# Dense projections issued as whole groups: a priority block around 21 of the 24 matmuls of each group

## The chip, the core and the metric

One core of one Trainium2 chip runs the whole program. The metric is the device time of one execution in microseconds, the median of several runs. The core has five engines that work side by side, each through its own queue in order: TensorE (PE) for matmuls, VectorE (DVE), ScalarE (ACT), GpSimd (POOL) and SyncE (SP), which here issues most of the DMAs. TensorE writes its results to PSUM, eight banks of 2 KB for each of 128 partitions; the other data lies in SBUF or in the chip's main memory.

## What is computed

The reference is one inference step of a two-layer decoder. Each layer normalises the hidden state, multiplies it by one input projection of 4108 columns, gives the columns to four mixers of four heads each, and multiplies the mixed result by an output projection:

```python
proj = jnp.einsum('btd,de->bte', hn, w_in_l)
...
s_hgrn, o_a = run_mixer(chunk_vector_decay, step_vector_decay, ...)
...
s_gdn, o_b = run_mixer(chunk_gated_delta, step_gated_delta, ...)
...
s_ssd, o_c = run_mixer(chunk_scalar_decay, step_scalar_decay, ...)
...
s_ret, o_d = run_mixer(chunk_scalar_decay, step_scalar_decay, ...)
...
y = jnp.concatenate([y_a, y_b, y_c, y_d], axis=-1)
out = jnp.einsum('bte,ed->btd', y, w_out_l)
```

The prompt has 2048 tokens behind 16 learned ones; eight sample sequences of one token each run beside it with states of their own. The four mixers are recurrences over tokens: HGRN2 (a), the gated delta rule (b), Mamba-2 (c) and retention (d). All data is 32-bit.

## The kernel before

Tokens stand in 17 tiles: tile 0 holds the 16 learned tokens and the eight samples in 40 rows, the others 128 tokens each. Two tiles make a block (the first block has tile 0 as well), and there are eight blocks. A layer runs in five stages, each a loop over blocks or tiles:

- `mixC` (Mamba-2), blocks 0 to 7.
- `denseB` (the projections of the gated delta rule), blocks 0 to 7, with `prepB` after every second block. Beside it the walk starts: `walkB`, a generator that carries the gated-delta state over all 65 pieces of 32 tokens. Each piece (`stepB`) is a chain: a read of the state on PE (`wo`), an addition on DVE (`wz`, line 1212), an update on PE (`tr<-wz,bkt`), and the new state on DVE (`sbd`, line 312), on which the next read waits. `hook` puts the next step of the walk into the program at set places of the stages.
- `mixA` (HGRN2), blocks 0 to 7, with the rest of the walk beside it. After the projections of a block come eight rounds of score matmuls (`sc<-aq,ak`, line 235 by way of `scores`), up to 64 matmuls of 64 x 32 in a round; between two rounds DVE scales `aq` and `ak` in place (lines 792 and 793).
- `mixD` (retention), blocks 0 to 7. Its outputs take their PSUM bank in turn from the pools `po` and `pwo`; the walk holds the one buffer of `pwo` for a tile at a time.
- `outproj`, tiles 0 to 16.

Each projection is exact to nearly full precision through three matmuls on parts: the weights and the activations are split into a high and a low part, and high x high, high x low and low x high are added up in PSUM. Over the contraction of 1024 in eight steps this makes a group of 24 matmuls into one PSUM buffer; the pool `pd` has two of them. `dense_cm` (lines 478 to 487) computes 128 columns for a whole block of 256 or 296 tokens, `dense_rows` (489 to 496) up to 512 columns for one tile; it is called by `dense_tm` and `outproj`. Behind a group its eviction follows, which reads the PSUM buffer.

The order of the instructions on each engine is not the program's. A planner lays it down beforehand, engine by engine: whenever an engine is free in the planner's own timing, it takes, of the instructions whose inputs are there, the one of the lowest rank. The rank is the running number in the program. Inside `tc.high_priority(offset=n)` the rank is that number less n, and the instructions of such a block do not move the running number on: the first one after it continues where the block began. Evictions, weight loads and `prepB` stand in `early()`, which is an offset of 3000 (line 194); some small GpSimd steps have 6000 (`POFF`). On the chip each engine then runs its queue in that order.

The core of a group, before:

```python
for d in range(8):
    T.matmul(ps, hi[:, d], b.xh[:, d, 0:b.n], start=(d == 0), stop=False)
    T.matmul(ps, hi[:, d], b.xl[:, d, 0:b.n], start=False, stop=False)
    T.matmul(ps, lo[:, d], b.xh[:, d, 0:b.n], start=False, stop=(d == 7))
with early():
    evict(full[:, 0:4 + b.n] if raw else ps)
```

Of the kernel before, what the change touches and what calls it, by code (L numbers as in the profile page):

```python
# [92 lines left out]
def body(tc, ctx, a, o, nch, depth, blks, off):  # L93
    nc = tc.nc
    V, S, G, T = nc.vector, nc.scalar, nc.gpsimd, nc.tensor
# [97 lines left out]
    def early():  # L193
        return tc.high_priority(offset=3000)

    def ptile(pool, tag):
        return pool.tile([128, 512], F32, tag=tag, name=tag)
# [280 lines left out]
    def dense_cm(w, b, evict, raw=False):  # L478
        hi, lo = w
        full = ptile(pd, "pd")  # L480
        ps = full[:, 4:4 + b.n]
        for d in range(8):
            T.matmul(ps, hi[:, d], b.xh[:, d, 0:b.n], start=(d == 0), stop=False)  # L483
            T.matmul(ps, hi[:, d], b.xl[:, d, 0:b.n], start=False, stop=False)  # L484
            T.matmul(ps, lo[:, d], b.xh[:, d, 0:b.n], start=False, stop=(d == 7))  # L485
        with early():
            evict(full[:, 0:4 + b.n] if raw else ps)

    def dense_rows(ps, R, pcs, xh, xl):
        nd, n = pcs[0][0].shape[1:3]  # L490
        for d in range(8):
            hi, lo = (x[:, d % nd] for x in pcs[d // nd])
            T.matmul(ps[0:R, 0:n], xh[:, d], hi, start=(d == 0), stop=False)  # L493
            T.matmul(ps[0:R, 0:n], xh[:, d], lo, start=False, stop=False)  # L494
            T.matmul(ps[0:R, 0:n], xl[:, d], hi, start=False, stop=(d == 7))  # L495
        return ps[0:R, 0:n]

    def dense_tm(pcs, b, evict):
        for t in b.tiles:
            R, x0 = rows(t), b.col[t]  # L500
            r = dense_rows(ptile(pd, "pd"), R, pcs, b.xh[:, :, x0:x0 + R], b.xl[:, :, x0:x0 + R])
            with early():
                evict(t, r)
# [29 lines left out]
    def dense_z(ws, b):  # L533
        z = blk("z")
        for p in range(2):
            dense_cm(ws[p], b, lambda ps: silu2(ps, z[:, p, 0:b.n], b.n))
        return z
# [173 lines left out]
    def mixA(L, W, b):  # L711
# [4 lines left out]
        for p in range(2):  # L716
            dense_cm(wq[p], b, lambda ps: silu2(ps, q[:, p, 0:n], n))
            hook(rA)
        for p in range(2):
            def evf(ps):  # L720
                th = we("th")
                act(th[:, 0:n], ps, AF.Tanh, scale=0.5)
                fo = f[:, p, 0:n]
                act(kk[:, p, 0:n], th[:, 0:n], AF.Identity, scale=L.lc[:, 4 + p:5 + p], bias=L.lc[:, 2 + p:3 + p])
                V.tensor_scalar(fo, th[:, 0:n], L.lc[:, 2 + p:3 + p], L.lc[:, p:p + 1], ALU.mult, ALU.add)
                V.tensor_scalar(fo, fo, TINY, None, ALU.max)
            dense_cm(wff[p], b, evf)
            hook(rA)
# [881 lines left out]
    def outproj(L, W, t, Ln, between=None):  # L1610
        R = rows(t)
        y = f4([128, 8, 128], "yf")
        nc.sync.dma_start(y[:, :, 0:R], ydr[t])
        yh, yl = xpair((NT - t) % 2, 128)
        S.copy(yh[:, :, 0:R], y[:, :, 0:R])
        tt(yl[:, :, 0:R], y[:, :, 0:R], f32(yh[:, :, 0:R]), ALU.subtract)
        hx = f4([128, D], "hx")
        load_h(L.l, t, hx)
        for qd in range(2):
            ps = dense_rows(ptile(pd, "pd"), R, W[qd], yh[:, :, 0:R], yl[:, :, 0:R])  # L1620
            cs = slice(512 * qd, 512 * qd + 512)
            tt(hx[0:R, cs], hx[0:R, cs], ps, ALU.add)  # L1622
            if between:
                with early():
                    next(between)
                    Wn = next(between)
        if Ln is not None:
            nc.sync.dma_start(hdr[t], hx[0:R])
            xprep(Ln, t, hx)
            if between:  # L1630
                return Wn
        else:
            stt(hx[0:R], hx[0:R], rms_scale(hx, R), fnw[0:R], ALU.mult, ALU.mult)
            if t == 0:
                nc.sync.dma_start(o["y_sample"].rearrange("b o d -> (b o) d"), hx[32:40])
            else:
                nc.sync.dma_start(o["y_prompt"][0, 128 * (t - 1):128 * t, :], hx)
# [158 lines left out]
```

## Time and profile before

| | us |
|---|---|
| median of three runs | 2864.69 (2863.39 to 2867.74) |
| the profiled execution | 2857.64 |
| its span, first to last instruction | 2855.9 |
| PE busy | 2734.7 |
| PE weight loads busy | 2483.6 |
| DVE busy | 1694.0 |
| ACT busy | 1010.5 |
| POOL busy | 1057.8 |

The page gives the busy time of each engine, its costliest groups of instructions and what ended the idle time ahead of them. The windows view gives the same by stretch of time, the timeline gives single instructions with start and length. Matmuls are pipelined, so a matmul of 0.28 us may have its successor start 0.12 us later; what the stream costs is read from the distance of starts.

### The profile page before, as it was taken

The numbers are of one execution on the slowest core, as the hardware profiler recorded it, in microseconds if no ns is written. First come the engines' busy times: TensorE is split into PE (matmuls) and PEld (weight loads), VectorE is DVE, ScalarE is ACT, GpSimd is POOL, SyncE is SP. The second block draws the span as 40 slices with busy tenths as digits, with TensorE's granted clock in tenths as the row PEclk, the third lists the DMA queues.
The fourth block names the chain that finished last, engine by engine and source line by source line (L and its number), as shares of the span: only waits on it lengthen the run. The fifth ranks groups of instructions, "written<-read, shape, count | busy, mean of one in ns | idle before, by whom it ended". The sixth has DMA issues, their size and how long they took to land. (4 is left out here: it accounts for less than half of the span.)

```text
span 2855.9 us, 72831 instructions
## 1 busy us (share of the span) xinstructions
PE 2734.7 (96%) x29492; PEld 2483.6 (87%) x29492; DVE 1694.0 (59%) x4756; ACT 1010.5 (35%) x2547; POOL 1057.8 (37%) x2032
## 2 busy tenths in 40 slices
PE   6989999989999999999988999899999999999998
PEld 6889898989889888888878999899988898888887
DVE  5777766655666745454456767656566657444533
ACT  4545532333333412232244445233333333222321
POOL 4454546557323221110033535646763322212100
PEclk9999999999999999999999999999999999999999
DMA  7243445563232423237772424534632223322443
GB/s 181 66 141 108 146 136 151 155 160 104 69 111 72 132 73 112 77 111 210 223 216 81 143 92 123 144 119 142 185 97 86 74 97 97 97 96 72 146 140 111
DMA packets 385175, 349.69 MB, mean 122 GB/s; under 512 B 144313, under 2 KB 349617, under 8 KB 374601
## 3 DMA queue, kind: packets, MB, share of 16 engines
q1 hardware_dynamic: 381320, 335.96, 38.3%
q0 software_dynamic: 3520, 9.09, 1.6%
q8 instruction: 233, 3.82, 0.5%
q14 instruction: 102, 0.83, 0.1%
HBM read 247.06 MB, written 98.10 MB: 121 GB/s over the span
## 5 line engine op out<-in xcount | busy, mean ns | idle before, releaser
L483 PE MATMUL pd<-xh,wh 128*128 128x256 f32 (+1 forms) x2816 | 825.7, 293 | 25.3 <-DVE hB L907 10.4
L484 PE MATMUL pd<-xl,wh 128*128 128x256 f32 (+1 forms) x2816 | 813.1, 289 | 0.0
L485 PE MATMUL pd<-xh,wl 128*128 128x256 f32 (+1 forms) x2816 | 811.8, 288 | 0.9 <-DVE wl L458 0.7
L483 PEld LDWEIGHTS pd<-xh,wh 128*128 128x128 f32 x2816 | 539.4, 192 | 43.1 <-issue 18.9
L493 PE MATMUL pd<-wh,xh 128*128 128x512 f32 (+5 forms) x1632 | 561.3, 344 | 7.0 <-DVE sraw L1354 5.8
L494 PE MATMUL pd<-wl,xh 128*128 128x512 f32 (+5 forms) x1632 | 558.5, 342 | 3.1 <-POOL wl L458 2.8
L495 PE MATMUL pd<-wh,xl 128*128 128x512 f32 (+5 forms) x1632 | 558.3, 342 | 0.1
L484 PEld LDWEIGHTS pd<-xl,wh 128*128 128x128 f32 x2816 | 539.1, 191 | 5.6 <-issue 3.9
L485 PEld LDWEIGHTS pd<-xh,wl 128*128 128x128 f32 x2816 | 539.1, 191 | 5.1 <-issue 2.4
L493 PEld LDWEIGHTS pd<-wh,xh 128*128 128x128 f32 (+1 forms) x1632 | 303.2, 186 | 47.4 <-issue 7.9
L494 PEld LDWEIGHTS pd<-wl,xh 128*128 128x128 f32 (+1 forms) x1632 | 303.3, 186 | 40.5 <-POOL wl L458 3.4
L495 PEld LDWEIGHTS pd<-wh,xl 128*128 128x128 f32 (+1 forms) x1632 | 303.1, 186 | 38.3 <-issue 1.7
L312 DVE TENSOR_TENSOR sbd<-low,tr 64x128 f32<-64x128 f32 x384 | 109.1, 284 | 134.5 <-PE tr L235 129.2
L335 POOL TENSOR_TENSOR fm<-fm,expo 128x4 f32<-128x4 f32 (+3 forms) x136 | 130.8, 962 | 81.5 <-DVE fm L612 73.8
L610 POOL TENSOR_SCALAR fm<-fm 128x4 f32<-128x4 f32 (+3 forms) x102 | 22.9, 225 | 340.7 <-DVE fm L607 315.3
L339 POOL TENSOR_SCALAR rm<-rm 128x1 f32<-128x1 f32 (+1 forms) x51 | 13.9, 273 | 339.6 <-ACT junk L357 338.8
L243 POOL COPY bwi<-wz 32x256 f32<-32x256 f32 x128 | 57.6, 450 | 215.3 <-DVE wz L1212 205.4
L1622 DVE TENSOR_TENSOR hx<-hx,pd 128x512 f32<-128x512 f32 (+1 forms) x68 | 46.6, 686 | 147.9 <-PE pd L495 147.8
L530 ACT ACTIVATE th<-pd 128x256 f32<-128x256 f32 (+2 forms) x162 | 62.4, 386 | 190.9 <-PE pd L485 152.6
L235 PEld LDWEIGHTS sc<-aq,ak 64*32 64x32 f32 (+1 forms) x7008 | 95.0, 108 | 39.4 <-issue 10.2
L235 PE MATMUL sc<-aq,ak 64*32 64x32 f32 (+1 forms) x7008 | 125.8, 199 | 2.8 <-ACT sq L783 1.3
L1116 POOL TENSOR_TENSOR bR<-bR,bW 128x120 f32<-128x120 f32 (+14 forms) x300 | 117.3, 391 | 21.1
(521 smaller groups left out, 5096.2 us busy)
## 6 DMA issues: line engine op xcount, KB each, us to landing
xh<-xh SPq DMA_DIRECT2D x56, 1024.0 KB
xl<-xl SPq DMA_DIRECT2D x56, 1024.0 KB
wr<-in_w_in_dram SPq DMA_DIRECT2D x64, 512.0 KB
hx<-in_x_prompt_dram SPq DMA_DIRECT2D x32, 512.0 KB
y<-y SPq DMA_DIRECT2D x128, 128.0 KB
yf<-y SPq DMA_DIRECT2D x32, 512.0 KB
bld<-qkv SPq DMA_DIRECT2D x32, 384.0 KB
xh<-xh SPq DMA_DIRECT2D x8, 1184.0 KB
```

The lines of the kernel that those rows point to most:

```text
L235: T.matmul(out, l, r, start=start, stop=stop, skip_group_check=True)
L243: G.tensor_copy(dst, src)
L312: tt(new[rr, :, hh], low[rr, :, hh], pv, ALU.add)
L335: G.tensor_tensor(dst, src, e.broadcast_to(list(src.shape)), ALU.pow)
L483: T.matmul(ps, hi[:, d], b.xh[:, d, 0:b.n], start=(d == 0), stop=False)
L484: T.matmul(ps, hi[:, d], b.xl[:, d, 0:b.n], start=False, stop=False)
L485: T.matmul(ps, lo[:, d], b.xh[:, d, 0:b.n], start=False, stop=(d == 7))
L493: T.matmul(ps[0:R, 0:n], xh[:, d], hi, start=(d == 0), stop=False)
L494: T.matmul(ps[0:R, 0:n], xh[:, d], lo, start=False, stop=False)
L495: T.matmul(ps[0:R, 0:n], xl[:, d], hi, start=False, stop=(d == 7))
L530: act(th[0:R, 0:n], ps, AF.Tanh, scale=0.5)
L1116: f(R_[0:2 * nu, 0:m, j + 1:32], R_[0:2 * nu, 0:m, j + 1:32], wv, ALU.subtract)
```

## The change

In both functions that hold the loop of a group, the three matmuls of each of the eight steps but the first are put into a priority block with an offset of 9000. The first three keep their rank. Nothing else is edited; each instruction and its operands are the same.

```diff
@@ dense_cm
         for d in range(8):
-            T.matmul(ps, hi[:, d], b.xh[:, d, 0:b.n], start=(d == 0), stop=False)
-            T.matmul(ps, hi[:, d], b.xl[:, d, 0:b.n], start=False, stop=False)
-            T.matmul(ps, lo[:, d], b.xh[:, d, 0:b.n], start=False, stop=(d == 7))
+            with tc.high_priority(offset=9000) if d else ExitStack():
+                T.matmul(ps, hi[:, d], b.xh[:, d, 0:b.n], start=(d == 0), stop=False)
+                T.matmul(ps, hi[:, d], b.xl[:, d, 0:b.n], start=False, stop=False)
+                T.matmul(ps, lo[:, d], b.xh[:, d, 0:b.n], start=False, stop=(d == 7))
@@ dense_rows
         for d in range(8):
             hi, lo = (x[:, d % nd] for x in pcs[d // nd])
-            T.matmul(ps[0:R, 0:n], xh[:, d], hi, start=(d == 0), stop=False)
-            T.matmul(ps[0:R, 0:n], xh[:, d], lo, start=False, stop=False)
-            T.matmul(ps[0:R, 0:n], xl[:, d], hi, start=False, stop=(d == 7))
+            with tc.high_priority(offset=9000) if d else ExitStack():
+                T.matmul(ps[0:R, 0:n], xh[:, d], hi, start=(d == 0), stop=False)
+                T.matmul(ps[0:R, 0:n], xh[:, d], lo, start=False, stop=False)
+                T.matmul(ps[0:R, 0:n], xl[:, d], hi, start=False, stop=(d == 7))
```

## Rows read from the trace of the kernel before

**Rows 1.** The page's first part: span, then busy time, share and instructions of PE

```profile
span 2855.9 us, 72831 instructions
PE 2734.7 (96%) x29492; PEld 2483.6 (87%) x29492; DVE 1694.0 (59%) x4756; ACT 1010.5 (35%) x2547; POOL 1057.8 (37%) x2032
```

**Rows 2.** Windows, layer 0's first four stages: busy us by engine, granted clock, DMA

```profile
0.00:344.00 344.00, 300.64 (x2279) 283.85 (x2280) 239.49 (x654) 173.48 (x428) 166.07 (x222) 0.97 0.44 132
344.00:645.00 301.00, 284.94 (x3435) 270.71 (x3435) 185.42 (x570) 102.64 (x273) 168.77 (x340) 0.98 0.52 146
645.00:1030.00 385.00, 378.87 (x6654) 342.60 (x6650) 248.95 (x790) 140.25 (x391) 144.78 (x379) 1.00 0.29 90
1030.00:1255.00 225.00, 223.54 (x1554) 197.40 (x1554) 115.38 (x313) 60.38 (x144) 42.66 (x64) 1.00 0.33 106
```

**Rows 3.** The page's costliest groups: busy us, mean ns, idle before

```profile
L483 PE MATMUL pd<-xh,wh 128*128 128x256 f32 (+1 forms) x2816 | 825.7, 293 | 25.3 <-DVE hB L907 10.4
...
L493 PE MATMUL pd<-wh,xh 128*128 128x512 f32 (+5 forms) x1632 | 561.3, 344 | 7.0 <-DVE sraw L1354 5.8
```

**Rows 4.** PE's timeline, four full-width matmuls within a dense group: start, length

```profile
2159.80 0.28 PE L484 MATMUL pd<-xl,wh 128*128 128x256 f32 x1
2159.92 0.61 PE L235 MATMUL tr<-wz,bkt 128*128 128x128 f32 x4
...
2160.48 0.28 PE L483 MATMUL pd<-xh,wh 128*128 128x256 f32 x1
```

**Rows 5.** PE's timeline, 4 and 64 score matmuls within a dense group

```profile
857.52 0.28 PE L485 MATMUL pd<-xh,wl 128*128 128x256 f32 x1
857.63 0.28 PE L483 MATMUL pd<-xh,wh 128*128 128x256 f32 x1
857.85 0.25 PE L235 MATMUL sc<-aq,ak 64*32 64x32 f32 x4
...
858.25 0.28 PE L485 MATMUL pd<-xh,wl 128*128 128x256 f32 x1
...
897.49 0.28 PE L483 MATMUL pd<-xh,wh 128*128 128x256 f32 x1
897.70 0.82 PE L235 MATMUL sc<-aq,ak 64*32 64x32 f32 x64
...
898.67 0.28 PE L485 MATMUL pd<-xh,wl 128*128 128x256 f32 x1
```

**Rows 6.** PE's timeline, what is not dense in 5 us of the HGRN2 stage

```profile
818.08 0.61 PE L235 MATMUL tr<-wz,bkt 128*128 128x128 f32 x4
818.53 0.61 PE L235 MATMUL tr<-cst,bgx 128*128 128x128 f32 x4
819.07 0.60 PE L235 MATMUL sc<-aq,ak 64*32 64x32 f32 x42
819.60 0.71 PE L235 MATMUL wo<-sbd,bnq 128*128 128x128 f32 x4
820.24 0.36 PE L235 MATMUL sc<-aq,ak 64*32 64x32 f32 x22
...
823.12 0.61 PE L235 MATMUL tr<-wz,bkt 128*128 128x128 f32 x4
```

**Rows 7.** DVE's timeline, the walk's addition ahead of the first of these updates

```profile
815.43 0.41 DVE L1212 TENSOR_TENSOR wz<-bwi,wo 32x256 f32<-32x256 f32 x1
```

**Rows 8.** PE's timeline, layer 0: the walk's last update and retention's first scores

```profile
1000.72 0.61 PE L235 MATMUL tr<-wz,bkt 128*128 128x128 f32 x4
...
1049.07 0.31 PE L235 MATMUL sc<-dqk 64*32 64x32 f32 x8
```

**Rows 9.** Windows, the edge between the second and the third stage of layer 0

```profile
600.00:612.00 12.00, 7.64 (x46) 7.60 (x47) 7.35 (x15) 6.85 (x13) 8.74 (x12) 0.63 0.69 205
```

**Rows 10.** PE's timeline, the two walk updates that lie closest

```profile
2390.65 0.60 PE L235 MATMUL tr<-wz,bkt 128*128 128x128 f32 x4
...
2393.59 0.71 PE L235 MATMUL tr<-wz,bkt 128*128 128x128 f32 x4
```

## What was predicted

> **What bounds the kernel now.** I read the page's first part before anything else: TensorE (PE) has work running for 2734.7 of 2855.9 us [rows 1], so 121 us of its time are empty and no other engine is near full. Then the busy time by stage in layer 0 [rows 2]: the third stage (HGRN2, with the gated-delta walk beside it) keeps PE at 378.9 of 385 us and the retention stage at 223.5 of 225; the two stages ahead of these have the holes, 43 and 16 us. Here the kernel is a stream of matmuls on one in-order queue, and its time is what the stream costs plus the holes. So I ask two things of the change: does it make the stream cheaper, and does it widen or close holes.
>
> The stream is mostly dense projections: 2816 and 1632 triples, 24 matmuls to a group [rows 3], so 4448 / 8 = 556 groups. I went through the timeline of PE group by group: 320 of the 556 have something else between their first and last matmul, in 437 runs, 394 of them behind the third matmul. The HGRN2 stage has a habit [rows 6]: every 5.0 us (818.08 to 823.12) one pair of a walk update (`tr<-wz`) and a walk read (`wo`), one batch of 64 score matmuls (here cut into 42 and 22), and 20 to 22 dense matmuls.
>
> **The change part by part.** No instruction is added or taken away; the same 29492 matmuls run. In this planner an instruction's rank is its place in the program less the offset, and what is traced in a priority block does not move the counter on. So 21 of 24 matmuls of each group now go as soon as PE is free and their weights are there, and nothing else on PE (walk, scores, transposes, the early preparation with its offset of 3000) is taken between them; the first three still wait their turn.
>
> *What an interruption costs on PE itself.* Within a group, starts are 0.12 us apart (857.52 to 857.63) [rows 5]. Four full-width matmuls put between two dense ones: 2159.80 to 2160.48 is 0.68 us for two dense steps (0.24) and the run, so 0.44 us for the run, 0.11 each [rows 4]. Four such matmuls cost 0.11 each in a run of their own kind too (818.08 to 818.53) [rows 6]. So a full-width run costs nothing for standing inside a group: term 1 is zero. A run on a part of the array is different: 4 score matmuls take 0.62 - 0.24 = 0.38 us and 64 take 1.18 - 0.24 = 0.94 us [rows 5], so each is worth 0.0093 us and entering and leaving together about 0.35 us. That is paid wherever such a run stands; it is saved only where two of them become one.
>
> *How many entries go.* Moving every run out of the body of its group to the group's end, in the order in which the rows stand, takes the entries into part-of-array runs from 358 to 348: 10 x 0.35 = 3.5 us. That is the floor. The ceiling: the HGRN2 scores run as 267 separate runs, while the loops ask for 124 batches, so 143 entries or 50 us would go if none were cut. But about half of the cuts have no dense matmul beside them; they come from walk runs that become ready while a batch is being issued (`wo` between 42 and 22 [rows 6]). Whole groups help there only because more work is waiting when a group ends, so that a batch is ready entire. I take 16 more entries, near the floor since the order within the waiting work is not what is edited: term 2 is 26 x 0.35 = -9 us, with -3.5 and -50 as its ends.
>
> *What waits longer.* A run that becomes ready inside a group now waits for its end: up to 21 x 0.12 = 2.5 us. Whether that costs anything is a matter of slack, and the timelines show it [rows 6, 7]: the walk's `wz` is finished at 815.84, and its update starts on PE at 818.08, 2.24 us later. Over the 129 updates of both layers, four start within 0.3 us of what they need. Most updates stand so, behind dense matmuls; with 24 in that place of 20 to 22 it moves by 0.3 to 0.5 us. Eight groups a block (six of 128 columns and two row tiles) meet eight score batches a block, so one whole group in each 5 us cycle is just what there is. The walk has room behind it: its last update of layer 0 starts at 1000.72, retention's first scores at 1049.07 [rows 8]. I price term 3 at zero, hidden by that slack and by the dense stream; without cover it is the slow rival below.
>
> *Evictions and weights.* Evictions keep their offset of 3000. Since a group ends sooner after it starts, they can only come sooner, which is worth at most the holes ahead of the first matmul of a group, 25.3 us at L483 and 7.0 at L493 in all [rows 3], and below nothing if three whole groups in a row outrun the two PSUM buffers; there the waiting runs fill PE. I take zero. As the counter is no longer moved on by 7/8 of the dense work, 3000 places reach back over about 5.5 HGRN2 blocks in place of 4.2, so weight loads on SP's queue may be issued earlier; the staging buffers are handed out in program order, so a weight tile can't take one from the walk. Zero, with 10 us either way at the stage edges.
>
> Sum against the profiled run's own 2857.64 us: -9. The median of the three runs is 7 us above that run, and I carry the difference over: 2864.69 - 9 = 2856 us.
>
> **A rule of the skill that bears on it.** TensorE's granted clock is 1.00 over the whole HGRN2 stage, where nearly every group is cut [rows 2], and 0.63 in the 12 us from 600, behind an empty PE between the second and the third stage [rows 9]; the level there is 1.2 GHz for a part of the time. Of the 13 slow stretches of the record, 71 us together, twelve stand behind holes or at the start and end; one (from 1919.5) stands behind a full PE, with many small matmuls on parts of the array. "TensorE: Matmul & The Clock Gate", section "Why this matters for your kernels", of the Trainium skill says that the loop nest decides whether matmuls stay warm, and gives as the good form one in which they stay back to back. By that rule whole groups would win back up to half of the 71 us, 36 us, against next to nothing by the rows: a cut group is not an idle one here.
>
> **The rivals.**
>
> *Nothing comes of it.* The order changes and the stream costs the same: only the floor of term 2 is met and holes shift by a few us either way. For it: full-width runs cost nothing in a group, and half of the cut score batches have no dense work beside them. Time 2861, within 0.2% (5.7 us, about what a measurement of this kernel can tell from no change).
>
> *The chains starve (slower).* Place: the HGRN2 stage, both layers. If an update misses the end of a group by a little, the next group's three ordinary matmuls go, and 21 more with them. Then one walk step takes two groups, one ahead of the update and one ahead of the read, and a block's eight groups are used up by four of its eight cycles. The other four run uncovered. The shortest cycle in the trace is 2.94 us from update to update (2390.65 to 2393.59), of which PE has about 1.85 of work (0.45, 0.94 and 0.44) [rows 10]; 1.1 us x 4 x 16 blocks is 70 us at most. With half of the blocks hit, +35: 2900 us. It decides from about 0.5 us of delay per visit, where that slack [rows 6, 7] and the length of a group meet. A walk that is late by 48 us or more also reaches retention's outputs, which share its PSUM bank [rows 8]. For it: every chain now waits in lumps of 2.5 us, 5 us in the 512-column groups. Against it: four tight updates of 129, and dense work that is not lost but done earlier.
>
> *The clock rises.* Chains held back in lumps, holes at stage edges closed, some slow stretches gone: half of the 36 us and half of the 25 us of group starts, -30: 2835 us. Against it: the holes with low clock are at edges between stages, where no dense group is ready.
>
> **How the numbers follow.** Forecast 2856, its own range 2846 to 2862: chance 0.45, of which 0.08 lies within 0.2%. Nothing comes of it: 0.16. Chains starve: 0.33, all slower. Clock rises: 0.06, all faster. So faster by over 0.2%: 0.37 + 0.06 = 0.43; within 0.2%: 0.08 + 0.16 = 0.24; slower: 0.33. Both signs hold weight, so the range reaches to the cases on either side: down to 2824 (the 10 us of edges and three fifths of term 2's ceiling, 30 us), up to 2905 (the slow rival's half with 5 us of edges). Left out are chains that starve in most blocks, and a gain near the whole ceiling.
>
> **What would show it.** Right: nearly no run inside a group behind its third matmul; PE's busy time nearly as before; fewer entries into score runs, with more batches whole at 64; the HGRN2 stage shorter than 385 us by 3 to 5. Wrong: PE waiting for `wz`, `sbd` or `ak` from DVE by more than 10 us in all; the walk's last update much later than 1000 us after the start; blocks of that stage longer than 48 us with the same dense count. A change of more than 15 us in the first two stages would say that evictions or weight loads, not the walk, are what moved, and that I looked in the wrong place.

## The result and the profile after

Before 2864.04 us (median of four runs), after 2951.22 us: ratio 1.030, 95% interval 1.0275 to 1.0325. The change costs 87 us. The profiled run after took 2950.93 us (span 2949.2), the one before 2857.64 (span 2855.9), so 93 us of span are to be explained.

The page's first part after, which answers [rows 1]:

```profile
span 2949.2 us, 72865 instructions
PE 2765.6 (94%) x29492; PEld 2514.4 (85%) x29492; DVE 1700.7 (58%) x4756; ACT 1011.5 (34%) x2547; POOL 1047.2 (36%) x2032
```

PE is empty for 183.6 us in place of 121.2 (span less busy), +62, and its busy time has risen by 31 us although the same 29492 matmuls run. So some of them ran slower. Windows show where. I cut both traces at the same events (each stage's first score matmul, then the first addition of the output projection, then the next layer's first scores): first stage, second stage, HGRN2, retention, and layer edge, all of layer 0. Columns: the window, its length, busy us of PE, PEld, DVE, ACT and POOL with counts, granted clock, DMA share, GB/s. Before:

```profile
0.00:351.00 351.00, 307.64 (x2335) 290.80 (x2336) 245.19 (x673) 177.39 (x444) 168.69 (x225) 0.97 0.44 130
351.00:645.00 294.00, 277.94 (x3379) 263.76 (x3379) 179.72 (x550) 98.73 (x258) 166.15 (x337) 0.98 0.53 148
645.00:1049.00 404.00, 396.57 (x6753) 357.31 (x6749) 257.26 (x816) 144.57 (x404) 149.75 (x387) 1.00 0.30 94
1049.00:1254.00 205.00, 204.84 (x1450) 182.23 (x1450) 106.39 (x285) 56.06 (x130) 37.45 (x56) 1.00 0.31 99
1254.00:1505.00 251.00, 234.27 (x1200) 196.41 (x1197) 115.33 (x202) 75.94 (x144) 40.71 (x53) 0.98 0.66 199
```

After, answering [rows 2]:

```profile
0.00:375.00 375.00, 313.76 (x2338) 296.81 (x2338) 247.93 (x678) 179.70 (x445) 167.09 (x222) 0.93 0.40 122
375.00:686.00 311.00, 282.62 (x3314) 268.51 (x3309) 183.74 (x543) 96.75 (x253) 167.72 (x332) 0.95 0.49 139
686.00:1115.00 429.00, 413.86 (x6903) 374.51 (x6900) 257.87 (x826) 146.82 (x411) 153.24 (x397) 0.98 0.30 92
1115.00:1313.00 198.00, 196.21 (x1366) 172.40 (x1367) 102.99 (x278) 55.35 (x128) 33.08 (x54) 0.99 0.31 99
1313.00:1582.00 269.00, 247.34 (x1255) 208.33 (x1253) 124.90 (x221) 79.32 (x157) 40.23 (x52) 0.95 0.63 193
```

The reader is to see two things. The loss is spread: +24, +17, +25, -7 and +18 us, the HGRN2 stage no more than the first. And the clock fell in each of these windows. At half the granted clock (0.50, the 1.2 GHz level) the trace has 182 us in 31 stretches, against 71 us in 13; ahead of 30 of the 31 PE has just been empty, for 0.9 to 4.6 us in sum over the last few microseconds. Not every hole brings one: of the 39 holes of 1 us or more after, 12 (1.1 to 2.2 us long) have no such stretch in them or within 7 us behind them. A stretch at that level costs about half of its length (a dense step 0.25 us instead of 0.14, shown below), so +111 us of it are about +55 us. Entries into part-of-array runs (runs of matmuls on 32 or 64 of the array's rows or columns) fell from 358 to 323, at 0.35 us each -12 us. Sum: 62 + 55 - 12 = 105 against 93; it is somewhat high, since an empty stretch at half clock counts twice in it. Of the time at half clock PE had work running in 134 us after and in 46 us before; with half of these 88 us the sum is 62 + 44 - 12 = 94.

Where PE is empty, by the costliest groups (answering [rows 3]) and by PE's waits:

```profile
L484 PE MATMUL pd<-xh,wh 128*128 128x256 f32 (+1 forms) x2816 | 838.6, 298 | 60.7 <-ACT wh L457 16.3
...
L495 PE MATMUL pd<-wh,xh 128*128 128x512 f32 (+5 forms) x1632 | 565.9, 347 | 7.3 <-ACT wh L457 2.2
```

After:

```profile
PE sc L235 <- POOL cgu L1367: 22.4, 11, 10.0
PE pd L484 <- ACT wh L457: 16.3, 4, 7.2
PE pd L484 <- ACT u L895: 14.2, 3, 11.2
PE tr L519 <- DVE hx L514: 13.8, 2, 10.9
PE sc L235 <- ACT sq L785: 8.4, 8, 1.6
```

Before, the copies `u`:

```profile
PE pd L483 <- ACT u L893: 5.1, 3, 3.5
```

(Columns of the waits: what waited for what, us in all, times, longest.) The idle time ahead of a 128-column group's first matmul went from 25.3 to 60.7 us, 35 of the 62. Few and long waits make half of the 60.7: 3 for a copy `u` out of PSUM (14.2 us, 5.1 before) and 4 for a weight copy `wh` (16.3 us; in the kernel before no 128-column group waited for it), both on ScalarE, up to 11.2 us.

[Rows 8] have moved too, the walk's last update of layer 0 by 59 us and retention's first scores by 66:

```profile
1059.79 0.60 PE L235 MATMUL tr<-wz,bkt 128*128 128x128 f32 x4
...
1114.64 0.32 PE L235 MATMUL sc<-dqk 64*32 64x32 f32 x8
```

**One hole from end to end.** The longest such wait, at the layer's edge (PE, start and length, idle before in brackets):

```profile
1540.09 0.30 PE L484 MATMUL pd<-xh,wh 128*128 128x296 f32 x1
1540.23 0.30 PE L485 MATMUL pd<-xl,wh 128*128 128x296 f32 x1
...
1543.78 0.60 PE L519 MATMUL tr<-ident,hx 128*128 128x128 f32 x4
1547.28 1.12 PE L519 MATMUL tr<-ident,hx 128*128 128x128 f32 x4 [2.90 <-DVE hx L514]
...
1549.47 0.45 PE L485 MATMUL pd<-xl,wh 128*128 128x296 f32 x1
1549.72 0.45 PE L486 MATMUL pd<-xh,wl 128*128 128x296 f32 x1
...
1554.51 0.30 PE L486 MATMUL pd<-xh,wl 128*128 128x296 f32 x1
1565.99 0.62 PE L484 MATMUL pd<-xh,wh 128*128 128x296 f32 x1 [11.18 <-ACT u L895]
```

ScalarE in the same microseconds, and SyncE's queue:

```profile
1549.69 1.08 ACT L524 CAST xth<-tr 128x512 fp32r<-128x512 f32 x2
1552.20 0.23 ACT L911 ACTIVATE th<-cb 128x32 f32<-128x32 f32 x1 [1.43 <-DVE cb L907]
1564.07 1.06 ACT L357 ACTIVATE junk<-hx 128x1024 bf16<-128x1024 f32 x1 [11.64 <-DMA xh<-xth]
...
1565.43 0.17 ACT L893 COPY u<-pd 128x32 f32<-128x32 f32 x1
```

```profile
1538.78 13.67 SPq L1306 DMA_DIRECT2D dgb<-smd  x6
1552.55 4.64 SPq L527 DMA_DIRECT2D xh<-xth  x2
```

`xprep`'s transposes (L519) are copied to `xth`; `xth` is stored by a DMA whose issue stands on SyncE until 1552.55; the scratch output `junk` of the next tile's sum of squares is a slot of the same ring of four as `xth`, so ScalarE waits 11.64 us for that store; the copies `u` that would empty PE's two PSUM buffers stand behind it in ScalarE's queue; PE is empty for 11.18 us. Ahead of the hole and behind it the dense steps are at half clock, 0.25 us instead of 0.14:

```profile
1549.00:1554.00 5.00, 4.95 (x20) 0.50 0.12 3
1554.00:1566.00 12.00, 0.82 (x7) 0.64 0.37 89
1566.00:1571.00 5.00, 5.00 (x20) 0.50 0.00 0
```

(Windows of PE alone: busy, granted clock, DMA share, GB/s.)

**The next longest.** Two of the weight copy's waits stand at the start of the HGRN2 stage, one in each layer:

```profile
643.18 0.62 PE L484 MATMUL pd<-xh,wh 128*128 128x296 f32 x1 [7.22 <-ACT wh L457]
642.08 1.04 ACT L457 CAST wh<-wr 128x1024 fp32r<-128x1024 f32 x1 [7.86 <-DMA wr<-in_w_in_dram]
635.84 4.57 SPq L450 DMA_DIRECT2D wr<-in_w_in_dram  x3
2088.53 0.62 PE L484 MATMUL pd<-xh,wh 128*128 128x296 f32 x1 [5.29 <-ACT wh L457]
```

Here ScalarE itself waits for the weight's DMA, which SyncE's queue issues only from 635.84 on. The kernel before had a hole of 6.58 us at this place too, in layer 0, behind `hB`. What holds the issue back was not tried.

### The profile page after: what moved, and what is told of

Read it like the earlier page. It is cut to its first block, busy times and chain, and to the rows that moved or that the text cites. A ratio compares the mean times of both kernels' runs of the same rounds, so it can differ in the third digit from the quotient of the medians.

```text
span 2949.2 us, 72865 instructions
## 1 busy us (share of the span) xinstructions
PE 2765.6 (94%) x29492; PEld 2514.4 (85%) x29492; DVE 1700.7 (58%) x4756; ACT 1011.5 (34%) x2547; POOL 1047.2 (36%) x2032
## 5 line engine op out<-in xcount | busy, mean ns | idle before, releaser
L484 PE MATMUL pd<-xh,wh 128*128 128x256 f32 (+1 forms) x2816 | 838.6, 298 | 60.7 <-ACT wh L457 16.3
L484 PEld LDWEIGHTS pd<-xh,wh 128*128 128x128 f32 x2816 | 547.8, 195 | 76.7 <-issue 19.4
L485 PEld LDWEIGHTS pd<-xl,wh 128*128 128x128 f32 x2816 | 547.8, 195 | 6.6 <-issue 5.6
L486 PEld LDWEIGHTS pd<-xh,wl 128*128 128x128 f32 x2816 | 547.1, 194 | 3.2 <-POOL wl L458 1.6
L235 PE MATMUL sc<-aq,ak 64*32 64x32 f32 (+1 forms) x7008 | 118.9, 199 | 12.8 <-ACT sq L785 8.4
L1117 POOL TENSOR_TENSOR bW<-bU,bR 128x120 f32<-128x120 f32 (+14 forms) x300 | 113.8, 379 | 37.7 <-DMA bR<-bscr 17.3
```

Of the source, the lines that this page charges most:

```text
L235: T.matmul(out, l, r, start=start, stop=stop, skip_group_check=True)
L1117: f(wv, bcm(U_[0:2 * nu, j, j + 1:32], 1, m), bcl(R_[0:2 * nu, 0:m, j], 31 - j), ALU.mult)
```

## The experiments

Each time is the median of its runs beside runs of the kernel before on the same chip. The span, empty time, time at half clock (h.c.) and entries into part-of-array runs are from the profiled execution.

| kernel | us | ratio [95%] | span | PE empty | h.c. | entries |
|---|---|---|---|---|---|---|
| before | 2864 | 1 | 2856 | 121 | 71 | 358 |
| after | 2951 | 1.030 [1.0275, 1.0325] | 2949 | 184 | 182 | 323 |
| e1_counter | 2887 | 1.0098 [1.0076, 1.012] | 2885 | 135 | 93 | 388 |
| e2_whole | 2953 | 1.0323 [1.0301, 1.0345] | 2947 | 186 | 163 | 326 |
| e3_cm | 2932 | 1.0249 [1.0221, 1.0276] | 2929 | 172 | 136 | 348 |
| e4_rows | 2905 | 1.0156 [1.0127, 1.0185] | 2901 | 147 | 111 | 378 |
| e5_half | 2893 | 1.0105 [1.0078, 1.0132] | 2893 | 141 | 118 | 347 |
| e6_tr | 2919 | 1.0197 [1.017, 1.0225] | 2915 | 162 | 125 | 325 |
| e7_walk | 2985 | 1.0427 [1.04, 1.0454] | 2981 | 189 | 213 | 367 |
| e8_mixA | 2990 | 1.0443 [1.04, 1.0485] | 2987 | 210 | 211 | 280 |
| e9_CB | 2914 | 1.0177 [1.0129, 1.0224] | 2918 | 162 | 131 | 339 |
| e10_gate | 2956 | 1.0334 [1.0313, 1.0354] | 2953 | 190 | 162 | 331 |
| e11_evict | 2962 | 1.0353 [1.0303, 1.0403] | 2961 | 194 | 180 | 332 |
| e12_weights | 2966 | 1.0367 [1.0302, 1.0433] | 2959 | 187 | 187 | 323 |
| e13_junk | 2928 | 1.0231 [1.02, 1.0263] | 2921 | 171 | 125 | 326 |
| n1_null | 2868 | 1.002 [1.0004, 1.0036] | 2866 | 127 | 77 | 359 |
| c1_before_walk | 2872 | 1.0047 [1.003, 1.0065] | 2866 | 120 | 88 | 374 |
| c2_tr | 2861 | 0.9995 [0.9977, 1.0013] | 2852 | 122 | 65 | 356 |
| c3_yield | 2871 | 1.0032 [1.0018, 1.0046] | 2869 | 122 | 86 | 387 |
| c4_junk | 2851 | 0.9962 [0.995, 0.9973] | 2849 | 115 | 77 | 358 |

In every row the change of the span is, within 17 us, the change of PE's empty time plus half of that at half clock plus 0.35 us an entry (e5_half: 20 + 23 - 4 = 39 against 37; e7_walk: 68 + 71 + 3 = 142 against 125). With only the half-clock time in which PE has work running it is within 7 us, but for e8_mixA (15).

Spans by stage, as changes against before (0 and 1 are the layers; "edge" runs from the output projection's first addition of layer 0 to layer 1's first scores, and with it goes layer 1's first stage):

| kernel | first 0 | second 0 | HGRN2 0 | ret. 0 | edge | first 1 | second 1 | HGRN2 1 | ret. 1 |
|---|---|---|---|---|---|---|---|---|---|
| after | +23 | +18 | +24 | -7 | +18 | -7 | +14 | +20 | -12 |
| e2_whole | +27 | +15 | +22 | -6 | +20 | -2 | +11 | +15 | -11 |
| e5_half | +2 | +5 | +19 | -9 | +7 | -2 | +10 | +13 | -10 |
| e6_tr | +5 | +14 | +19 | -5 | +7 | +1 | +11 | +17 | -10 |
| e7_walk | +27 | +14 | +31 | -6 | +20 | -2 | +24 | +28 | -10 |
| e8_mixA | +26 | +1 | +43 | +3 | +14 | -3 | +17 | +31 | -3 |
| e13_junk | +22 | +15 | +19 | -7 | -19 | +15 | +16 | +13 | -10 |

### Which part of the change costs

**The running number alone.** The blocks are there with offset 0: groups can be cut as before, and what is traced in them no longer moves the number on.

```diff
-            with tc.high_priority(offset=9000) if d else ExitStack():
+            with tc.high_priority(offset=0) if d else ExitStack():
```

> The priority blocks are kept, but with an offset of 0: the running number is still not moved on by the 21 matmuls, and their rank is that of their place, so groups can be cut as before. Theory 1, whole groups make the chains on PE wait in lumps: 2855 to 2875 us, near the kernel before, and PE's holes near 121 us. Theory 2, the shorter running number gives evictions, weight loads and the early preparation a longer reach and so another order on all engines: 2935 to 2960 us.

**Whole groups alone.** The offset is 9000 and the number is moved on by three for each block, in both functions, so all other work keeps its rank.

```diff
                 T.matmul(ps, lo[:, d], b.xh[:, d, 0:b.n], start=False, stop=(d == 7))
+            for _ in range(3 if d else 0):
+                tc.tile_snap_priority()
```

> The offset of 9000 stays, and the running number is moved on by three after each block, so that everything else has exactly the rank of the kernel before. Theory 1 (lumps): 2930 to 2960 us, with PE's holes near 180 us and the walk's last update of layer 0 near 1060 us. Theory 2 (counter): 2850 to 2875 us.

Measured: 2887 and 2953 us. Whole groups without the shortened number cost what the whole change costs; the number by itself costs 25 us, with 30 more entries and 22 us more at half clock, but not on top of whole groups. The first lies outside both of its ranges; why the number costs 25 alone is left open. The following kernels start from this second one.

**One kind of group whole,** the 128-column groups of `dense_cm` (e3) or the row groups of `dense_rows` (e4); the other function is that of before:

```diff
     def dense_cm(w, b, evict, raw=False):
...
+            with tc.high_priority(offset=9000) if d else ExitStack():
...
     def dense_rows(ps, R, pcs, xh, xl):
...
         for d in range(8):
             hi, lo = (x[:, d % nd] for x in pcs[d // nd])
             T.matmul(ps[0:R, 0:n], xh[:, d], hi, start=(d == 0), stop=False)
```

(e3; e4 has the block in the second and not in the first.)

> Whole groups, with the running number moved on, in dense_cm alone (352 of the 556 groups, 2.9 us each); dense_rows as before. Theory 1: most of the loss, 2915 to 2945 us, since these groups stand in all four mixer stages. Theory 2: 2855 to 2875 us.

> Whole groups, with the running number moved on, in dense_rows alone (204 groups, of which 68 are the output projection's); dense_cm as before. Theory 1: a small loss, 2865 to 2895 us, since few chains stand beside these groups. Theory 2: 2855 to 2875 us.

Measured: 2932 and 2905 us. Both cost, in different places: e3 +25 and +27 in the second stages and +1 at the edge, e4 +10 and +10 there and +19 at the edge, where the output projection is made of row groups. That is more than was expected of e4.

**Half groups.**

```diff
-            with tc.high_priority(offset=9000) if d else ExitStack():
+            with tc.high_priority(offset=9000) if d % 4 else ExitStack():
```

> Whole groups halved: of the eight steps of a group, steps 1 to 3 and 5 to 7 have the priority, steps 0 and 4 are ordinary, and the running number goes on as before. A ready run then waits at most for 9 matmuls (9 x 0.12 = 1.1 us) in place of 21 (2.5 us). Theory (chains wait for lumps): the loss falls with the length of a lump. Proportional to it: 9/21 of the 91 us of the whole groups, +39, 2900 us. If only waits beyond a slack count, less: 2870 to 2890. Rival (any re-planning of this order costs tens of us, whatever the lump): no fall, 2930 to 2950.

Measured: 2893 us, +31 of +91. As a whole the loss falls with the length of the lump (0.34 of it for 9 matmuls of 21, which is 0.43). By stage it does so in layer 0's first two stages and at the edge, 14 us in place of 62 (e2); HGRN2 and retention together keep 13 of 20.

**A null change** in the kernel before:

```diff
     def early():
-        return tc.high_priority(offset=3000)
+        return tc.high_priority(offset=2900)
```

> The kernel before with one number changed: the early block's offset is 2900 in place of 3000. No group is whole, and nothing that a theory speaks of is changed. It measures what a small re-planning does to this kernel by itself. Theory (the lumps cost the time): within 6 us of the kernel before, 2857 to 2869. Rival (the order is so finely balanced that nearly any re-planning costs 20 us or more): 2880 or later.

Measured: 2868 us, +7, at the edge of what was expected and a thirteenth of the change's effect. But e1, which is also a new plan with no group whole, costs 25 us. So how much a new order costs by chance is known from few kernels only, and differences of up to some 25 us between the kernels below rest on the places in their traces, not on the time alone.

### What the whole groups hold up

**The transposes for the next layer go first.** Here and below, `now` puts one instruction ahead of everything and moves the number on.

```diff
+    def now(f, *x, **kw):
+        with tc.high_priority(offset=20000):
+            f(*x, **kw)
+        tc.tile_snap_priority()
...
-                T.transpose(pv[:, d, 0:R], hx[0:R, 512 * q + 128 * d:512 * q + 128 * d + 128], ident[0:R, 0:R])
+                now(T.transpose, pv[:, d, 0:R], hx[0:R, 512 * q + 128 * d:512 * q + 128 * d + 128], ident[0:R, 0:R])
```

> Whole groups with the running number kept (the 2952 us kernel), and the eight transposes that prepare a tile for the next layer ahead of everything on PE. Theory: at the layer's edge (+20 us) these transposes stand behind whole groups of the output projection, and the copies out of PSUM of the next layer's first groups stand behind them on ACT; with the transposes first the edge gives back 15 to 20 us: 2930 to 2937. Rival: the edge's hole is ACT's own order, or a DMA's time, and the transposes are ready no earlier: 2948 to 2955.

Measured: 2919 us, 34 us back, more than expected: 13 at the edge and 22 in layer 0's first stage, which makes its own tiles by the same function. PE's wait ahead of the 128-column groups fell from 56.1 to 36.3 us.

```profile
L489 PE MATMUL pd<-xh,wh 128*128 128x256 f32 (+1 forms) x2816 | 830.3, 295 | 36.3 <-ACT wh L462 12.5
```

**The walk goes first** (`now` at each matmul and transpose of `keysB`, `stepB` and `blocks32`), then **the HGRN2 layer's own chains** (`now` at each one of `mixA`), then **the first two stages' chains** together with the transposes (`now` in `mixC`, `conv_samples`, `conv_out` and `prepB`). One line of each:

```diff
-                mm(X.wo[:, c0 + 128 * p:c0 + 128 * p + 128], X.nq[:, p, 128 * (bb // 2):128 * (bb // 2) + 128],
+                now(mm, X.wo[:, c0 + 128 * p:c0 + 128 * p + 128], X.nq[:, p, 128 * (bb // 2):128 * (bb // 2) + 128],
...
-                                mm(pv[j0:j0 + h, hh, c, p], kk[rr, p, cc:cc + h], q[rr, p, cc + w:cc + w + h],
+                                now(mm, pv[j0:j0 + h, hh, c, p], kk[rr, p, cc:cc + h], q[rr, p, cc + w:cc + w + h],
...
-                            mm(pv[32 * bb:32 * bb + 32, hh, y, p], k[rr, p, cc], m[rr, p, cc],
+                            now(mm, pv[32 * bb:32 * bb + 32, hh, y, p], k[rr, p, cc], m[rr, p, cc],
```

> Whole groups with the running number kept (the 2952 us kernel), and every matmul and transpose of the gated-delta walk ahead of everything else on PE. A walk step that is ready inside a group runs inside it, as in the kernel before; all else still waits for the group's end. Theory: the HGRN2 stage (+22 and +15 us) is late for the walk's sake and gives most of it back, the other stages stay: 2910 to 2925, and the walk's last update of layer 0 stands at about 1030 us after the start or earlier (1060 with whole groups). Rival: the stage is late for the wait of its own scores, outputs and evictions: 2940 to 2955.

> Whole groups with the running number kept (the 2952 us kernel), and every matmul and transpose of the HGRN2 layer's own (scores, outputs, updates, key transposes) ahead of everything else on PE; the walk waits for group ends as before. Theory: the HGRN2 stage is late (+22 and +15 us) because its own score batches wait, eight a block, each behind a group; it gives most of this back: 2920 to 2932. Rival: letting the walk in cost 32 us and freed nothing, so it is the same here: the stage's extra time is dense work that came over from the retention stage, holes and slow clock at its edges, and runs that are let into groups cost entries into part-of-array runs (0.35 us each): 2945 to 2975, with more such entries than 326.

> Whole groups with the running number kept, and ahead of everything else on PE the transposes for the next layer (as in the 2919 us kernel) together with the matmuls and transposes of the first stage (state-space scores, decays, convolution transposes) and of the second stage's preparation. The HGRN2 stage and the walk are left waiting. Theory: the first two stages' holes are chains that wait for groups, so their share (+5, +14 and +11 us over before in the 2919 us kernel) goes: 2885 to 2900. Rival: these holes stand behind GpSimd, ScalarE and weights that are late for another reason: 2912 to 2930.

Measured: 2985, 2990 and 2914 us. The first two are worse than whole groups alone, by 32 and 38 us, and the HGRN2 stages longer, not shorter; the third is 5 us below e6, within its interval. In e7 the walk comes back into the groups: 41 more entries (14 us) and 50 us more at half clock (25). In e8 PE is empty for 24 us more. Both are slower than theory and rival allowed, and e8's entries fell from 326 to 280 where more were expected. So letting the walk or the scores through gives nothing back. That their waiting costs nothing is not shown by it, since each edit brings costs of its own. What does stand out in the HGRN2 stages are stretches of over 4 us in which PE starts no dense matmul: 68 and 54 us in the two stages before, 112 and 108 in e2, 83 and 80 in e5, 108 and 107 in e7, 114 and 109 in e8. Whole groups use up a block's dense work ahead of its chains.

**Whole groups that start later** (in `mixA` the first three matmuls 300 places later), and **the change turned round** (the kernel before, all dense matmuls of `mixA` 300 places later), and **the walk first in the kernel before** (the edits of e7 without whole groups). The first two:

```diff
-            with tc.high_priority(offset=9000) if d else ExitStack():
+            with tc.high_priority(offset=9000) if d else tc.high_priority(offset=-300) if late[0] else ExitStack():
...
+            with tc.high_priority(offset=-300) if late[0] else ExitStack():
```

(`late[0]` is 1 within `mixA`'s dense calls.)

> Whole groups with the running number kept (the 2952 us kernel), and in the HGRN2 layer the first three matmuls of each group take a rank 300 places later (less than half a block), so that a whole group starts only when no other work of those 300 places is ready. Theory (whole groups use a block's dense work up ahead of its chains, and the end of the block runs uncovered): the time that PE spends in stretches of over 4 us without a dense matmul, 112 and 108 us in the two HGRN2 stages with whole groups (68 and 54 before), falls below 90 in each, and the stages give back 15 us or more of +22 and +15: 2915 to 2937. Rival (the chains lose by waiting inside the group, wherever it starts): the stages stay, 2945 to 2965.

> The kernel before, with the edit turned round: no group is whole, and all dense matmuls of the HGRN2 layer stand 300 places later, so that its chains go first and its dense work lasts longer. Theory (cover): the stretches without a dense matmul shorten from 68 and 54 us and the kernel gains a little, 2840 to 2858, against more entries into part-of-array runs (0.35 us each, 358 before). Rival: the HGRN2 stage is full as it is (7 and 10 us empty), later groups only delay what their evictions feed: 2865 to 2900.

> The kernel before, with every matmul and transpose of the gated-delta walk ahead of everything else on PE; groups as they were. With whole groups this cost 32 us. Theory (the order of the walk against the layer's own chains matters, not only the lumps): it costs here too, 2870 to 2895, through more entries and slower clock. Rival (it cost there only because whole groups had used the cover up): within 8 us of before.

Measured: 2956, 2871 and 2872 us. Starting later gave nothing back (those stretches 108 and 115 us). The turned change shortened them to 33 and 39 us, as the theory of cover said, and still cost 9 us: 29 more entries are 10 us. Nor do the uncovered stretches measure the loss: e3 has 106 and 97 us of them and its HGRN2 stages are 12 and 4 us longer, e5 has 83 and 80 and they are 19 and 13 longer. So they come with whole groups, and taking them away is not shown to gain. The walk first costs 11 us beside cut groups and 32 beside whole ones.

**Evictions first, weight splitting first:**

```diff
-        with early():
+        with tc.high_priority(offset=20000):
             evict(full[:, 0:4 + b.n] if raw else ps)
...
-            S.copy(hv[:, :, c0:c1], r)
+            now(S.copy, hv[:, :, c0:c1], r)
```

(e11, in `dense_tm` too; e12, at the subtraction behind the copy too.)

> Whole groups with the running number kept (the 2952 us kernel), and the work that empties a group's PSUM buffer (copies, tanh and what is traced with them) has the offset 20000 in place of 3000. Theory (two PSUM buffers are outrun: PE's waiting ahead of the first matmul of a 128-column group rose from 25 to 56 us, with ScalarE named for 32 of it): evictions go ahead of other ready work on ScalarE and VectorE, this waiting falls below 40, and the kernel gives back 15 to 35 us: 2915 to 2937. Rival: ScalarE is not busy with other work but stands behind an instruction that waits for a DMA or for PE, and a rank does not move that: 2943 to 2960.

> Whole groups with the running number kept, and the splitting of each weight tile (the copy on ScalarE and the subtraction on VectorE or GpSimd) ahead of everything else on its engine. Theory: part of PE's waiting ahead of a group (15 us named for the weight copy) is the copy standing behind other work on ScalarE; it falls below 5 and 10 to 20 us come back: 2932 to 2942. Rival: the copy waits for its DMA (ScalarE stands 52 us there, 36 before) or for a weight buffer that the group before still uses, and with the higher rank it only holds the evictions up: 2948 to 2975.

Measured: 2962 and 2966 us, nothing back. The wait ahead of a group is 60.1 us in e11 (56.1 in e2):

```profile
L484 PE MATMUL pd<-xh,wh 128*128 128x256 f32 (+1 forms) x2816 | 837.4, 297 | 60.1 <-ACT wh L457 16.9
```

My reading: a rank moves no instruction past one that already stands ahead of it in its queue and waits on the chip; in e11 the scratch copy `junk` still waits 82.0 us for the store, 12.1 at the longest. That led back to the hole at the edge.

**The wait in ScalarE's queue taken away.** The scratch of the sum of squares is written over the tile `y` that the output projection has just used, not to a slot of `xth`'s ring.

```diff
-        junk = w2([128, D], "junk", BF16)
+        junk = w2([128, D], "junk", BF16) if scr is None else scr
...
-            xprep(Ln, t, hx)
+            xprep(Ln, t, hx, scr=y.rearrange("p d c -> p (d c)"))
```

> Whole groups with the running number kept (the 2952 us kernel), and at the layer's edge the scratch output of the sum of squares (junk) is written over the tile of mixer outputs that has just been used, in place of a slot in the ring that it shares with the transposed tiles xth and xtl. Theory: at the edge ScalarE stands up to 12.2 us ahead of this instruction, until the store of xth frees its slot (80 us in 13 waits in all), and PE's next groups stand behind the evictions queued after it. With another place for it these waits go, the edge gives back 10 to 20 of its 20 us, 2930 to 2942. Rival: ScalarE then stands at the next instruction for the same data, and PE's hole stays: 2946 to 2958.

> The kernel before with the same other place for that scratch output; groups as they were. ScalarE stands 70 us in 13 waits there, the longest 6.1 us. Theory: at the layer's edge PE has 17 us empty and 9 us of slow clock, and part of it stands behind these waits: 2850 to 2859. Rival: these waits are covered by dense work in the kernel before: within 4 us of it.

Measured: 2928 us with whole groups, 25 us back, and 2851 us with groups as before: 0.9962 [0.995, 0.9973], a version a little faster than both kernels. The gain is about twice what the null change moved the time the other way (1.002), so it rests on the trace as much as on the time. In the trace before ScalarE stood 69.9 us for the store, in the trace after 78.1:

```profile
ACT junk L357 <- DMA xh<-xth: 69.9, 13, 6.1
...
ACT junk L357 <- DMA xh<-xth: 78.1, 13, 11.6
```

In e13's waits that row is gone; the scratch waits only for its own input, and for 0.5 us a copy waits for the ring:

```profile
ACT junk L357 <- DVE hx L1628: 19.6, 2, 9.8
...
ACT xth L528 <- DMA xh<-xth: 0.5, 1, 0.5
```

The edge with the first stage behind it goes from +18 us in e2 to -4: 22 of the 25 us are there. In c4 the same two spans are 15 us shorter and 9 us longer, 6 of the 7 us by which its span is shorter, and PE is empty for 7 us less, with its busy time as it was:

```profile
span 2849.3 us, 72851 instructions
PE 2734.7 (96%) x29492; PEld 2487.1 (87%) x29492; DVE 1698.8 (60%) x4756; ACT 1011.8 (36%) x2547; POOL 1052.3 (37%) x2032
```

So the edge's loss is settled: with the shared ring whole groups lengthen the edge and the first stage behind it by 18 us (e2 against before), without it by 2 (e13's -4 against c4's -6). PE's order sets when the transposes come, and e6 shows that 13 us of the edge can be had there too; what turns a late transpose into a hole is a ring slot shared by a scratch tile and a stored one, on an in-order engine ahead of PE's evictions. A kernel with both edits, e6's and e13's, was not tried. c2_tr, the transposes first in the kernel before, moved nothing there:

> The kernel before, groups as they were, with one change: the eight transposes that prepare a tile for the next layer go ahead of everything else on PE. Theory: they take 34 us off where groups are whole; in the kernel before they wait at most for a few matmuls of lower rank, and PE's 17 us of waiting before them is for their data, so little is left: 2850 to 2862. Rival: their rank was late already in the kernel before, and the layer's edge (17 us empty, 9 us slow) gives back 10 us or more: 2850 or less.

Measured: 2861 us.

## Why the prediction was wrong

It forecast 2856 us, range 2824 to 2905; the kernel took 2951. By its steps:

- **What bounds the kernel** (the stream plus the holes): held, and it is the account in which the loss closes. The question "does it widen holes" was the right one and was answered for one place only.
- **Term 1** (a full-width run costs nothing inside a group): nothing in the runs speaks against it; PE's 31 us of longer busy time are what half clock adds (44) less the entries (12).
- **Term 2** (26 entries, -9 us): 35 entries fewer, -12 us by the same price. Right in kind and size, though 16 of the 26 were an estimate without a working of its own. The runs inside groups are gone as said: behind the third matmul, one of 556 groups is cut.
- **Term 3** (what waits longer, priced at zero by slack): failed. Additions `wz` that PE picks up within 0.3 us rose from 4 to 25, PE's waits for `wz`, `sbd` and `ak` are 19 us in all (7 before), above the 10 us named as a sign, and the walk's last update stands 59 us later. Of this only about 20 us of loss stay in HGRN2 and retention together (e2: +22 - 6 and +15 - 11). The slow rival, +35, had the place and the order of size of that part, but its cause is not borne out: letting the walk through whole groups made the stage longer.
- **Evictions** (zero, "there the waiting runs fill PE"): failed, and with the weights, below, the largest mis-sized term. The wait ahead of 128-column groups rose by 35 us, 9 of them for the copies `u` on ScalarE. I bounded it by [rows 3] as if groups alone decided when a buffer is emptied, and did not ask what stands ahead of the copy in ScalarE's queue. In the kernel before that scratch already waited 70 us for the store, most of it under cover of the dense work.
- **Moved work of low rank**: the prediction named walk, scores and transposes as held back and priced only the walk. The next layer's transposes alone were 34 us (e6).
- **Weights and the running number** (zero, ±10 us): the number alone moved 25 us, and nothing beside whole groups. PE's waits for the weight copy, 16 of the 35 us, were put at nothing, since loads "may be issued earlier"; whole groups made PE wait for them (14.9 us in e2, where the number is kept).
- **The clock**: the missing term. The prediction's own row showed twelve of 13 slow stretches behind holes or at the ends [rows 9], and used it only for a gain. Read the other way, a new hole is often paid twice: +62 us of holes brought +111 us at half clock, 55 us by half of it, 44 by PE's working time in it. The rule drawn from "TensorE: Matmul & The Clock Gate" of the Trainium skill, section "Why this matters for your kernels", that matmuls kept back to back stay warm, was read as a gain for whole groups; by the trace it was none, 182 us at half clock for 71: the groups were dense, and PE stood empty more ahead of them (35 us more in [rows 3]'s first group).
- **The sign set down beforehand** (a change of more than 15 us in the first two stages would say that evictions or weight loads moved, "and that I looked in the wrong place"): it came, +23 and +18 us.

Shown by experiment: about 40 of e2's 91 us, 22 in the first stage by the transposes (e6) and 18 at the edge with the stage behind it by the ring (e13). Left open: about 46, in the second stages (+26, where the weight waits of 7.2 and 5.3 us stand) and in HGRN2 with retention (+20). Five experiments that put one thing first (e7 to e9, e11, e12) did not give them back. No version with a third PSUM buffer, and none with the weights' DMAs issued earlier, was tried.

## What to carry to other kernels

Before ranking one engine's work higher, list everything of lower rank on that engine, follow each item to the queue it feeds, and look there for in-order instructions that wait for a DMA; a step that is covered today is the one that a lump uncovers. Price a hole on TensorE as its own length plus half of the slow-clock stretch behind it, where one follows. Let no scratch output share a ring with tiles that are stored by DMA: moving it was worth 0.4% here, and no change of order was.

## What was not expected of the hardware

The clock followed holes of a few microseconds in sum: 30 of the 31 half-clock stretches after stand behind a PE that had just been empty, and a stretch, up to 13.7 us long, is often longer than its hole. Two stretches (1919.5 before, 2001.1 after) stand behind a PE that the profile counts as busy throughout. Both follow the same run of small matmuls (first line before, second after):

```profile
1916.27 1.95 PE L235 MATMUL tr<-hones,bsq 128*128 128x2 f32 x16
...
1999.18 1.95 PE L235 MATMUL tr<-hones,bsq 128*128 128x2 f32 x16
```

Four more stretches after (670.0, 1891.9, 2069.4, 2113.8), with only 0.9 to 1.5 us of empty PE ahead of them, stand behind such matmuls too, 8 or 16 of them. It is not enough by itself: of the six runs of 16 before, one is followed by a stretch. So empty time and this run go together in some of the stretches; which of the two counted there is open.
